# A two-layer decoder on one core: a broadcast product placed later in the list, one filling step kept back in the last attention group, and one weight conversion shared between two engines

## The chip, the cores and the metric

The kernel runs on one core of a Trainium2 chip. The core has a matrix engine (TensorE, PE in the views, with its weight loads as PEld), VectorE (DVE), ScalarE (ACT), GpSimd (POOL) and SyncE (SP), which only issues transfers here. Each engine runs its own list of instructions in order, and an instruction that waits for another engine holds up all that stands behind it in its list. The metric is the device time of one execution in microseconds (us), the median of several runs.

## The reference

The input is 256 tokens of 1024 features. Two layers follow each other, and each has an attention and a gated feed-forward part.

```python
for l in range(2):
    h = rmsnorm(x, attn_norm[l])              # x * rsqrt(mean(x*x) + eps) * gain
    # layer 0: q, k, v from w_qkv_a, 16 heads, causal attention over the block of 256
    # layer 1: 16 query heads, 4 shared key/value heads, window 128, a learned sink per head
    x = x + o @ w_o
    h = rmsnorm(x, ffn_norm[l])
    u = conv3(h @ w_up[l])                    # causal depthwise convolution of width 3
    gate, val = split(u)                      # 2816 columns each
    x = x + (silu(gate) * val) @ w_down[l]
out = rmsnorm(x, final_norm)
```

All arrays are float32, and so is the result.

## The kernel before

**Split products.** Every large product runs on parts: a value v becomes hi, its rounding to a shorter float32 form (fp32r), and lo = v - hi. Three matmuls (hi·hi, hi·lo, lo·hi) then stand for one. The small products of the attention, and the transposes, run on plain float32; each of those is shown as two matmuls in the trace (L486, L463 and L715 have twice as many there as the list has).

**Weights.** The weights are packed into units of 128 x 2048 values. Each is fetched by SP (`fetch`), ScalarE makes the high part (L157, `hi_part`) and VectorE the low part (L160, `lo_part`), in two or four pieces per unit. High and low parts have four buffers each, so unit i + 4 can only be converted when unit i has been used up: `used(i)` calls `prepare(i + 4)`, which puts the pieces into the planner. Units 55 to 58 are the output projection of layer 1; units 59 and up are the up-projection of its feed-forward part, of which 59 to 62 are converted while units 55 to 58 are being used up.

**The planner.** The list of instructions is written out in the order in which the code runs. A clock in nanoseconds counts matmul work: `tick(ns)` adds the cost of what was just written, and then runs all put-off steps that have come due. `chain(key, (delay, step), ...)` puts a step off until its delay has passed on that clock, counted from the step before it. `require(key)` runs the steps of a key at once, when something needs them.

**The order on the engines.** Up to L498 the list is taken as it stands for PE, ACT, DVE and SP. Behind that point (`manual.close()`), a scheduler walks over the list, and gives each engine the earliest instruction of the list whose operands and buffers are ready by its own reckoning. So an instruction whose operand is late slides behind a few of its successors, and one that is ready can be taken ahead of one that is not. The order that comes out is fixed; on the chip each engine goes through it and waits where it has to.

**The start.** `first_parts(c)` prepares chunk c (of eight) of the first product: one transfer brings 128 x 256 values of x and 128 x 512 of the weights. ScalarE makes x's high part (`hi`, L783), VectorE x's low part (`lo`, L786) and the weights' low part (`wl`, L787). The weights' high part (`wh`) is made by VectorE for chunk 0 (L782), and by ScalarE for the others (L785). `v_first(c)` then has six matmuls of 512 columns at L739: two with hi and wh, two with lo and wh, two with hi and wl. GpSimd works out the rotary angles at the same time (L764 and on).

**1 / rms for the feed-forward part.** Behind an attention, the sums of squares of the two halves b = 0, 1 of the tokens give r = 1 / rms per token (`rstd_of`, its power on GpSimd at L303). `row_bcast` has to turn this column into a row that is the same on all partitions: VectorE multiplies the unit matrix by r (L719), PE multiplies a matrix of ones with that (`spread`, L715), and ScalarE copies the result into `rb` (L717). Both layers do it, while PE is in the first two blocks of the up-projection (`ffn`, L627 to L629; three matmuls of 256 columns between two ticks of 320 ns). These first blocks use unscaled values; `rb` scales their results (L656) and the values that later blocks take (L640, then L642 and L643), from block 4 on.

**Attention.** `attention` handles four groups of four heads. Per group it writes the scores, the softmax, for each of two pairs the transposes of the probabilities (`probs_T`, L463, copied by VectorE at L471 and ScalarE at L469), and the product with the values (`values`, L486), whose result ScalarE splits at L492 and VectorE at L493. Between these it calls `fill(ns)`, which adds ns to a budget and takes steps from `filler` until the budget is used up. In layer 1 the filler is first the query projections of groups 1 to 3 (48 steps of 320 ns), then units 55 to 57 of the output projection (`Down.units`, 12 steps of 1280 ns, each of six matmuls of 512 columns: L533, L534, L538). `lead` and `rate(g)` are those budgets: 3500 ahead of the groups, then three numbers per group, ahead of the first transposes, ahead of the second, and behind them. What the filler still has behind the last group is written there. Then `finish` has unit 58, which needs the last group's L492 and L493, adds the result to x (L603), transposes it (L264), and scales and splits it (L276, L279, L280) for the feed-forward part.

Of the kernel before, what the change touches and what calls it, by code (L numbers as in the profile page):

```python
# [10 lines left out]
AF = mybir.ActivationFunctionType  # L11
# [5 lines left out]
S = 256  # L17
# [43 lines left out]
def trunk(ctx: ExitStack, tc, x, xw, pos, cpk, fin, sinks, w, out):  # L61
    nc = tc.nc
# [25 lines left out]
    def row3(n=3 * P):  # L88
        return wk.tile([P, 3 * P], F32, tag="m3", name=nm("m3"), bufs=8)[:, :n]

    def bank(tag):
        return ps.tile([P, 512], F32, tag=tag, name=nm(tag), bufs=4 if tag == "acc" else 2)

    def f(ap):
        return ap.bitcast(F32)

    def blk(b):
        return slice(b * P, (b + 1) * P)
# [17 lines left out]
    def tick(ns):  # L116
        clock[0] += ns
        while put_off and not busy[0]:
            item = min(put_off, key=lambda t: t[0])
            if item[0] > clock[0]:  # L120
                return
            run_item(item)

    def chain(key, *steps, urgent=0):

        def run(k):
            if urgent:
                with tc.high_priority(offset=urgent):
                    steps[k][1]()
            else:  # L130
                steps[k][1]()
            if k + 1 < len(steps):
                put_off.append((clock[0] + steps[k + 1][0], key, lambda: run(k + 1)))
        put_off.append((clock[0] + steps[0][0], key, lambda: run(0)))
# [67 lines left out]
    def chunk(c):  # L202

        t, at = (first[c // 2], KC * (c < 2) + c % 2 * CH) if c < 6 else (first[c - 3], 0)
        return t[:, at:at + S], t[:, at + S:at + CH]
# [90 lines left out]
    def rstd_of(b):  # L296

        require("sq", b)
        st = sums[b]
        r = wk.tile([P, 1], F32, tag="rstd", name=nm("rstd"), bufs=6)  # L300
        nc.vector.tensor_tensor(out=st[:, 2:3], in0=st[:, 0:1], in1=st[:, 1:2], op=ALU.add)
        nc.vector.tensor_scalar(out=st[:, 3:4], in0=st[:, 2:3], scalar1=1.0 / D, scalar2=EPS, op0=ALU.mult, op1=ALU.add)
        nc.gpsimd.tensor_tensor(out=r, in0=st[:, 3:4], in1=mhalf, op=ALU.pow)  # L303
        return r

    def hx(hT, c):
        hi, lo = hT[c // 4]
        return hi[:, c % 4], lo[:, c % 4]
# [399 lines left out]
    def row_bcast(rb, b):  # L708

        r = rstd_of(b)  # L710
        d = row3(P)

        def spread():
            t = bank("t")
            nc.tensor.matmul(t[:, :P], ones, d, start=True, stop=True)  # L715
            tick(450)
            chain(("rb", b), (200.0, lambda: nc.scalar.activation(rb[:, blk(b)], t[:, :P], AF.Copy)))  # L717

        chain(("rb", b), (2000.0, lambda: nc.vector.tensor_scalar(out=d, in0=ident, scalar1=r, scalar2=None, op0=ALU.mult)),  # L719
              (300.0, spread))  # L720

    manual = ExitStack()
    manual.enter_context(tc.manual_schedule(engines={mybir.EngineType.PE, mybir.EngineType.Activation,
# [53 lines left out]
    def first_parts(c):  # L777
        hi, lo = hx(hT, c)
        (src, raw), g = chunk(c), (g1 if c > 1 else g0)[:, c:c + 1]
        wh, wl = (t[:, (c % 4) * 512:(c % 4 + 1) * 512] for t in wq[c // 4])  # L780
        if c == 0:
            nc.vector.tensor_copy(wh, raw)  # L782
        nc.scalar.activation(hi, src, AF.Copy, scale=g)  # L783
        if c > 0:
            nc.scalar.activation(wh, raw, AF.Copy)  # L785
        nc.vector.scalar_tensor_tensor(out=lo, in0=src, scalar=g, in1=f(hi), op0=ALU.mult, op1=ALU.subtract)  # L786
        nc.vector.tensor_tensor(out=wl, in0=raw, in1=f(wh), op=ALU.subtract)  # L787

    warm_up(8)
    for c in range(4):  # L790
        first_parts(c)
        v_first(c)
        if c % 2:
            fetch(2 + c // 2)
    for b in range(NB):
        nc.sync.dma_start(xr[b], x[blk(b)])
    for c in range(4, KC):
        first_parts(c)
        if c < KC - 1:
            v_first(c)  # L800
# [51 lines left out]
    mask = one.tile([P, S], F32, name="mask")  # L852
# [12 lines left out]
    qk = {}  # L865
# [49 lines left out]
    def after_a(b, n):  # L915
        chain(("sq", b), (1500.0, lambda: square(b, n)))
        if n == 1:
            chain(("rb", b), (1500.0 + 700.0, lambda: row_bcast(rb, b)))
        feats(b, n, [(hT, G_FFN[0])], ("x", b, n), y)
# [27 lines left out]
    qk = {}  # L947
# [5 lines left out]
    def q_group(g):  # L953
        q = quad()
        for b in range(NB):
            o = bank("acc")[:, :256]
            yield from proj(o, qT_h, b, cols256(U_QB + g), (U_QB + g,) if b else ())
            rotate(o, 2, b, q[:, 0:2], q[:, 2:4], ("qk", g), lambda t, b=b, o=o: q_out(t, b, o))
        qk[g] = (q[:, 0:2], q[:, 2:4], kT[:, 0:2], kT[:, 2:4], lambda p: g // 2, lambda p: diagonal(0)(g // 2))
# [4 lines left out]
    def filler_b():  # L964
        for g in range(1, 4):
            yield from q_group(g)
        yield from o_down[0].units(0, 3)
# [1 line left out]
    def ready_b(oT):  # L969
        o_down.append(Down(U_OB, 4, oT, lambda i: require("o", i)))  # L970

    attention(qk, ready_b, filler_b(), 3500.0, lambda g: ((4200.0, 2200.0, 1400.0), (3200.0, 1800.0, 1200.0), (3200.0, 1800.0, 1200.0), (4000.0, 1800.0, 1500.0))[g], mask, lambda h: 2 * (h // 8) + h % 2, True)

    hT = new_hT()
    y = [quad(F32, "y") for _ in range(2)]
# [1 line left out]
    def after_b(b, n):  # L977
        chain(("sq", b), (1500.0, lambda: square(b, n)))
        if n == 1:
            chain(("rb", b), (1500.0 + 700.0, lambda: row_bcast(rb, b)))  # L980
        feats(b, n, [(hT, G_FFN[1])], ("x", b, n), y)
# [138 lines left out]
```

## Time and profile before

| what | us |
|---|---|
| runs before | 571.11, 571.14, 572.1 |
| median | 571.14 |
| the profiled execution, its own time | 570.39 |
| its span from the first to the last instruction | 568.3 |
| PE busy | 558.8 |
| DVE busy | 427.1 |
| ACT busy | 380.0 |
| POOL busy | 100.3 |

The span leaves out about 2 us around the instructions. The views of the trace count time from the span's start. PE is the engine that is busy nearly all the time; a stretch in which it waits is seen in the list of its instructions as a start that comes later than the pace of its neighbours.

### The profile page before, as it was taken

The numbers are of one execution on the slowest core, as the hardware profiler recorded it, in microseconds if no ns is written. First come the engines' busy times: TensorE is split into PE (matmuls) and PEld (weight loads), VectorE is DVE, ScalarE is ACT, GpSimd is POOL, SyncE is SP. The second block draws the span as 40 slices with busy tenths as digits, with TensorE's granted clock in tenths as the row PEclk, the third lists the DMA queues.
The fourth block names the chain that finished last, engine by engine and source line by source line (L and its number), as shares of the span: only waits on it lengthen the run. The fifth ranks groups of instructions, "written<-read, shape, count | busy, mean of one in ns | idle before, by whom it ended". The sixth has DMA issues, their size and how long they took to land.

```text
span 568.3 us, 10191 instructions
## 1 busy us (share of the span) xinstructions
PE 558.8 (98%) x3858; PEld 504.5 (89%) x3858; DVE 427.1 (75%) x927; ACT 380.0 (67%) x768; POOL 100.3 (18%) x124
## 2 busy tenths in 40 slices
PE   8999999999999999999999999999999999999995
PEld 7888888899999999988888988879999999988884
DVE  6798678599788888744469988788898888773414
ACT  6988777578577776743449798877667777663313
POOL 7321001011333321100002200001333332110003
PEclk9999999999999999999999999999999999999999
DMA  8974344442565565664542714242466655565201
GB/s 326 374 277 154 144 148 149 149 149 76 213 216 202 206 211 213 217 203 177 219 148 96 276 76 149 74 149 76 149 223 223 221 206 198 230 221 205 92 0 74
DMA packets 15311, 100.99 MB, mean 178 GB/s; under 512 B 1952, under 2 KB 2080, under 8 KB 3744
## 3 DMA queue, kind: packets, MB, share of 16 engines
q1 hardware_dynamic: 14976, 100.09, 48.4%
q8 instruction: 30, 0.49, 0.3%
q10 hardware_dynamic: 288, 0.26, 0.1%
q14 instruction: 17, 0.14, 0.1%
HBM read 99.30 MB, written 1.05 MB: 177 GB/s over the span
## 4 chain that ended last, share of the span: by engine, by line
PE 88%; DVE 5%; ACT 4%; issue 1%; POOL 1%; DMA 1%; DVEq 0%; POOLq 0%; ACTq 0%
PE acc L533 9%; PE acc L538 9%; PE acc L534 9%; PE u L628 6%; PE u L629 6%; PE u L627 6%; PE t L628 6%; PE t L629 6%; PE t L627 6%; PE acc L317 4%; PE acc L319 4%; PE acc L318 4%; PE acc L739 2%; PE acc L628 2%; PE acc L629 2%; PE acc L627 2%
## 5 line engine op out<-in xcount | busy, mean ns | idle before, releaser
L160 DVE TENSOR_TENSOR wl<-wr,wh 128x1024 fp32r<-128x1024 f32 (+1 forms) x208 | 221.0, 1080 | 68.1 <-ACT wh L157 67.7
L157 ACT ACTIVATE wh<-wr 128x1024 fp32r<-128x1024 f32 (+1 forms) x208 | 190.0, 946 | 75.0 <-PE acc L538 55.4
L533 PE MATMUL acc<-wh,q 128*128 128x512 f32 x238 | 94.5, 397 | 0.8 <-ACT q L492 0.7
L534 PE MATMUL acc<-wl,q 128*128 128x512 f32 x238 | 92.9, 390 | 0.0
L671 POOL TENSOR_TENSOR m<-m,m 128x256 f32<-128x256 f32 x44 | 60.2, 1367 | 182.2 <-DVE m L666 109.2
L628 PE MATMUL u<-q,wh 128*128 128x256 f32 x320 | 88.5, 277 | 0.0
L627 PE MATMUL u<-q,wh 128*128 128x256 f32 x320 | 88.2, 276 | 0.0
L629 PE MATMUL u<-q,wl 128*128 128x256 f32 x320 | 88.1, 275 | 0.0
L629 PE MATMUL t<-q,wl 128*128 128x256 f32 x288 | 79.2, 275 | 0.0
L627 PE MATMUL t<-q,wh 128*128 128x256 f32 x288 | 79.2, 275 | 0.0
L628 PE MATMUL t<-q,wh 128*128 128x256 f32 x288 | 79.2, 275 | 0.0
L538 PE MATMUL acc<-wh,q 128*128 128x512 f32 x238 | 76.9, 389 | 0.0
L628 PEld LDWEIGHTS u<-q,wh 128*128 128x128 f32 x320 | 60.1, 188 | 0.1
L627 PEld LDWEIGHTS u<-q,wh 128*128 128x128 f32 x320 | 60.0, 188 | 0.1
L629 PEld LDWEIGHTS u<-q,wl 128*128 128x128 f32 x320 | 60.1, 188 | 0.0
L317 PE MATMUL acc<-wh,q 128*128 128x512 f32 (+1 forms) x160 | 57.1, 357 | 0.0
L319 PE MATMUL acc<-wh,q 128*128 128x512 f32 (+1 forms) x160 | 55.4, 346 | 0.0
L318 PE MATMUL acc<-wl,q 128*128 128x512 f32 (+1 forms) x160 | 55.2, 345 | 0.0
L627 PEld LDWEIGHTS t<-q,wh 128*128 128x128 f32 x288 | 54.1, 188 | 0.0
L628 PEld LDWEIGHTS t<-q,wh 128*128 128x128 f32 x288 | 54.1, 188 | 0.0
L629 PEld LDWEIGHTS t<-q,wl 128*128 128x128 f32 x288 | 54.1, 188 | 0.0
L533 PEld LDWEIGHTS acc<-wh,q 128*128 128x128 f32 x238 | 44.7, 188 | 10.5 <-ACT q L492 1.6
(165 smaller groups left out, 995.1 us busy)
## 6 DMA issues: line engine op xcount, KB each, us to landing
wr<-in_w SPq DMA_DIRECT2D x90, 1024.0 KB, 4.8
first<-in_xw SPq DMA_DIRECT2D x5, 384.0 KB, 5.6
xr<-in_x SPq DMA_DIRECT2D x2, 512.0 KB, 8.3
first<-in_xw SPq DMA_DIRECT2D x1, 768.0 KB, 7.0
fin_t<-in_fin SPq DMA_DIRECT2D x1, 512.0 KB, 6.2
out<-ot SPq DMA_DIRECT2D x1, 512.0 KB, 2.6
first<-in_xw SPq DMA_DIRECT2D x1, 388.0 KB, 3.6
out<-m ACTq DMA_DIRECT2D x1, 256.0 KB, 2.1
```

What stands on the lines that cost most here:

```text
L157: nc.scalar.activation(wq[i][0][:, c], raws[i][:, c], AF.Copy)
L160: nc.vector.tensor_tensor(out=wq[i][1][:, c], in0=raws[i][:, c], in1=f(wq[i][0][:, c]), op=ALU.subtract)
L317: nc.tensor.matmul(o, xh[:, blk(b)], wh, start=(c == 0), stop=False)
L318: nc.tensor.matmul(o, xh[:, blk(b)], wl, start=False, stop=False)
L319: nc.tensor.matmul(o, xl[:, blk(b)], wh, start=False, stop=(c == KC - 1))
L533: nc.tensor.matmul(o, ph[:, blk(b)], hi[:, s_], start=first, stop=False)
L534: nc.tensor.matmul(o, ph[:, blk(b)], lo[:, s_], start=False, stop=False)
L538: nc.tensor.matmul(o, pl[:, blk(b)], hi[:, s_], start=False, stop=end)
L627: nc.tensor.matmul(o, hi[:, s_], xh, start=(c == 0), stop=False)
L628: nc.tensor.matmul(o, hi[:, s_], xl, start=False, stop=False)
L629: nc.tensor.matmul(o, lo[:, s_], xh, start=False, stop=(c == KC - 1))
L671: nc.gpsimd.tensor_tensor(out=h, in0=gs, in1=t[1], op=ALU.mult)
```

## The change

Three places change. In `row_bcast` the step that holds the product with the ones is put off by 1500 ns on the planner's clock behind the multiplication of the unit matrix, and not by 300 ns; this holds in both layers. In `first_parts` the high part of chunk 1's weights is made in two halves: columns 0 to 255 by ScalarE, columns 256 to 511 by VectorE, where the copy stands ahead of the two low parts of that chunk. In layer 1 the last group's three filling budgets become 3600, 1200 and 600 ns instead of 4000, 1800 and 1500 ns.

```diff
@@ row_bcast
         chain(("rb", b), (2000.0, lambda: nc.vector.tensor_scalar(out=d, in0=ident, scalar1=r, scalar2=None, op0=ALU.mult)),
-              (300.0, spread))
+              (1500.0, spread))
@@ first_parts
         if c == 0:
             nc.vector.tensor_copy(wh, raw)
         nc.scalar.activation(hi, src, AF.Copy, scale=g)
-        if c > 0:
+        if c == 1:
+            nc.scalar.activation(wh[:, :S], raw[:, :S], AF.Copy)
+            nc.vector.tensor_copy(wh[:, S:], raw[:, S:])
+        elif c > 1:
             nc.scalar.activation(wh, raw, AF.Copy)
         nc.vector.scalar_tensor_tensor(out=lo, in0=src, scalar=g, in1=f(hi), op0=ALU.mult, op1=ALU.subtract)
@@ attention of layer 1
-    attention(qk, ready_b, filler_b(), 3500.0, lambda g: ((4200.0, 2200.0, 1400.0), (3200.0, 1800.0, 1200.0), (3200.0, 1800.0, 1200.0), (4000.0, 1800.0, 1500.0))[g], mask, ...)
+    attention(qk, ready_b, filler_b(), 3500.0, lambda g: ((4200.0, 2200.0, 1400.0), (3200.0, 1800.0, 1200.0), (3200.0, 1800.0, 1200.0), (3600.0, 1200.0, 600.0))[g], mask, ...)
```

## Rows read from the trace of the kernel before

**Rows 1.** The page: the busy time of each engine in us, with its share of the span, and the chain of work that ended last by engine.

```profile
PE 558.8 (98%) x3858; PEld 504.5 (89%) x3858; DVE 427.1 (75%) x927; ACT 380.0 (67%) x768; POOL 100.3 (18%) x124
PE 88%; DVE 5%; ACT 4%; issue 1%; POOL 1%; DMA 1%; DVEq 0%; POOLq 0%; ACTq 0%
```

**Rows 2.** The chain of waits, over the whole span, the two longest of PE's behind the start: who waited for whom, us in total, how often, the longest.

```profile
PE acc L533 <- ACT q L492: 0.7, 1, 0.7
PE t L715 <- DVE m L719: 0.6, 2, 0.3
```

**Rows 3.** The timeline in layer 0 around the two products with the ones (L715): start us, duration us, engine, line, operation, tiles, shapes, count, and in brackets the idle time before it and what ended it.

```profile
122.14 1.12 POOL L303 TENSOR_TENSOR rstd<-st,mhalf 128x1 f32<-128x1 f32 x1 [0.38 <-DVE st L302]
122.32 0.28 PE L629 MATMUL acc<-q,wl 128*128 128x256 f32 x1
122.44 0.43 PE L715 MATMUL t<-m,ones 128*128 128x128 f32 x2
122.62 0.36 PE L627 MATMUL acc<-q,wh 128*128 128x256 f32 x1
...
123.18 0.28 PE L628 MATMUL u<-q,wh 128*128 128x256 f32 x1
123.30 0.29 DVE L719 TENSOR_SCALAR m<-ident,rstd 128x128 f32<-128x128 f32 x1 [0.45 <-POOL rstd L303]
123.74 0.46 PE L715 MATMUL t<-m,ones 128*128 128x128 f32 x2 [0.28 <-DVE m L719]
123.95 0.36 PE L629 MATMUL u<-q,wl 128*128 128x256 f32 x1
```

**Rows 4.** The timeline in layer 1 at the same place, columns as before.

```profile
386.02 0.28 PE L628 MATMUL acc<-q,wh 128*128 128x256 f32 x1
386.28 0.46 PE L715 MATMUL t<-m,ones 128*128 128x128 f32 x2
386.50 0.36 PE L629 MATMUL acc<-q,wl 128*128 128x256 f32 x1
...
387.06 0.28 PE L627 MATMUL u<-q,wh 128*128 128x256 f32 x1
387.18 0.29 DVE L719 TENSOR_SCALAR m<-ident,rstd 128x128 f32<-128x128 f32 x1 [0.44 <-POOL rstd L303]
387.61 0.46 PE L715 MATMUL t<-m,ones 128*128 128x128 f32 x2 [0.27 <-DVE m L719]
387.82 0.36 PE L628 MATMUL u<-q,wh 128*128 128x256 f32 x1
```

**Rows 5.** The timeline in layer 1's attention: the values of the last group but one (the first two rows), and the end of the last group, PE, ACT and DVE.

```profile
360.75 1.52 PE L486 MATMUL t<-m,v 128*64 128x256 f32 x16
362.20 0.49 PE L533 MATMUL acc<-wh,q 128*128 128x512 f32 x1
...
368.64 0.39 PE L533 MATMUL acc<-wh,q 128*128 128x512 f32 x1
370.00 0.81 PE L463 MATMUL u<-ident,m 128*128 128x128 f32 x6
370.20 1.15 ACT L157 ACTIVATE wh<-wr 128x512 fp32r<-128x512 f32 x2 [0.89 <-PE acc L538]
370.75 1.90 PE L486 MATMUL t<-m,v 128*64 128x256 f32 x16
371.00 2.57 DVE L160 TENSOR_TENSOR wl<-wr,wh 128x512 fp32r<-128x512 f32 x4
371.25 0.47 ACT L469 ACTIVATE m<-u 128x384 f32<-128x384 f32 x1
371.62 1.14 ACT L157 ACTIVATE wh<-wr 128x512 fp32r<-128x512 f32 x2
372.68 0.60 ACT L492 ACTIVATE q<-t 128x512 fp32r<-128x512 f32 x1
373.33 0.50 PE L533 MATMUL acc<-wh,q 128*128 128x512 f32 x1 [0.69 <-ACT q L492]
```

**Rows 6.** The timeline of the start, chunks 0 and 1: POOL, ACT, DVE and PE.

```profile
4.38 0.43 DVE L782 CAST wh<-first 128x512 fp32r<-128x512 f32 x1 [3.32 <-DMA first<-in_xw]
5.22 1.19 POOL L764 TENSOR_SCALAR rb<-rb 128x8 f32<-128x8 f32 x2
6.06 0.73 PE L739 MATMUL acc<-wl,q 128*128 128x512 f32 x2
6.10 0.62 ACT L785 ACTIVATE wh<-first 128x512 fp32r<-128x512 f32 x1
6.22 0.49 DVE L786 SCALAR_TENSOR_TENSOR q<-first,q 128x256 fp32r<-128x256 f32 x1 [0.22 <-ACT q L783]
6.75 0.69 DVE L787 TENSOR_TENSOR wl<-first,wh 128x512 fp32r<-128x512 f32 x1
6.77 1.18 PE L739 MATMUL acc<-wh,q 128*128 128x512 f32 x4
8.24 0.39 PE L739 MATMUL acc<-wh,q 128*128 128x512 f32 x1
```

**Rows 7.** Instructions by line: duration in ns as shortest, median and longest, and when the first and the last start.

```profile
L279 DVE CAST q<-y x16: 282/284/295, 114.2 to 384.2; 128x256 fp32r<-128x256 f32 x16
L717 ACT ACTIVATE rb<-t x4: 277/278/278, 122.9 to 388.1; 128x128 f32<-128x128 f32 x4
```

More of the change, by code (lines that the diff above doesn't have):

```diff
@@ L970, in ready_b @@
         o_down.append(Down(U_OB, 4, oT, lambda i: require("o", i)))
-    attention(qk, ready_b, filler_b(), 3500.0, lambda g: ((4200.0, 2200.0, 1400.0), (3200.0, 1800.0, 1200.0), (3200.0, 1800.0, 1200.0), (4000.0, 1800.0, 1500.0))[g], mask, lambda h: 2 * (h // 8) + h % 2, True)
+    attention(qk, ready_b, filler_b(), 3500.0, lambda g: ((4200.0, 2200.0, 1400.0), (3200.0, 1800.0, 1200.0), (3200.0, 1800.0, 1200.0), (3600.0, 1200.0, 600.0))[g], mask, lambda h: 2 * (h // 8) + h % 2, True)
     hT = new_hT()
```

## Prediction, made before the changed kernel ran

> **What bounds the kernel now.** I read the page first: PE is busy 98% of the span, and the chain that ended last runs through PE for 88% of its length [rows 1]. Time can then be won only where PE has nothing to do, or does something it needn't. So I read next the chain of waits for PE alone. Behind the start it names two places: L533, which waits 0.7 us once for the copy L492, and the product with the ones, L715, which waits 0.6 us in two instances for VectorE's L719 [rows 2]. These are small beside 571 us, and the list counts only what ends a wait, not what a late start costs the instructions behind it. So I read each place in the timeline and compare the distance between starts with the pace of an undisturbed neighbour: both layers around L715 [rows 3, 4], the end of layer 1's last attention group [rows 5], and the start, where PE is not yet fed [rows 6]. The three edits lie at exactly these places; whether each gives back its stall is the question.
>
> **Part 1: the product with the ones.** In layer 0 the starts in the undisturbed list are 0.12 us apart (122.32 to 122.44). The first product costs 122.62 - 122.32 - 0.12 = 0.18 us: the work itself and the change of type. The second costs 123.95 - 123.18 - 0.12 = 0.65 us, so 0.47 us of it is waiting. What it waits for is L719, which starts at 123.30, right behind GpSimd's power that took from 122.14 to 123.26 [rows 3]. In layer 1 the first costs 386.50 - 386.02 - 0.12 = 0.36 us and the second 387.82 - 387.06 - 0.12 = 0.64 us [rows 4], that is 0.18 and 0.46 us over an undisturbed one. Together 0.47 + 0.18 + 0.46 = 1.11 us of waiting.
>
> How much later does the product come? The up-projection ticks 320 ns for three matmuls. With 300 ns the step falls due one such triple behind L719's, with 1500 ns five triples behind it (1600 ns): four triples, 12 matmuls, later in the list. The second keeps its place one triple behind the first. In the compiled order of before the scheduler had already slid both back a little, for lack of their operand, by 3 and 5 matmuls in layer 0, so that on the engine the second moves by 12 - 5 = 7 matmuls at least, 7 x 0.12 = 0.84 us, and by 12 at most, 1.44 us. PE, which could have been at it at 123.30, is then there at 124.1; the operand, 0.15 us behind the end of L719 at 123.59, is there at 123.74. The margin is 0.3 to 0.4 us, in layer 1 the same or one matmul more. So all 1.11 us should go; bounded by 0 (the operand moves with PE) and 1.11 us.
>
> What is late next: the copies into `rb` (L717), by some 0.3 us for the second one, since the product itself starts at 124.1 and not at 123.74. Queued behind them on ScalarE and VectorE are L640, L642 and L656; their result is needed from block 4 of the up-projection, more than 10 us later (three blocks of 48 matmuls are between). No transfer and no queue of SP or POOL is passed. I cost it at nothing; the cover is those blocks, and it would have to shrink by 10 us.
>
> **Part 2: half of chunk 1's high weights on VectorE.** PE starts chunk 1 at 6.77, right behind ScalarE's `wh`, which runs from 6.10 to 6.72; PE's own work of chunk 0, two matmuls that started at 6.06, would let it go on at about 6.5 [rows 6]. ScalarE takes 0.62 us for 512 columns [rows 6] and 0.28 for 128 [rows 7]; on a line between them half the columns take 0.39 us. Then `wh` is whole at 6.5 instead of 6.72, if VectorE has its half by then. It stands idle for 0.22 us ahead of L786 [rows 6], and a conversion of 128 x 256 takes it 0.28 us [rows 7]: it delays L786 by under 0.1 us, and PE needs that only behind two matmuls. The low part (6.75 to 7.44) is needed behind four matmuls, 4 x 0.23 = 0.9 us after 6.55, at 7.45, so it costs at most 0.1 us. From 8.24 on PE is fed. Gain 0.2 us; bounds 0 and 6.77 - 6.51 = 0.26 us.
>
> GpSimd runs two instructions from 5.22 to 6.41, right where VectorE's new copy would start (about 6.0); the only such conversion that the start shows, at 4.38, took 0.43 us while GpSimd was between instructions [rows 6], so no row shows one that starts in the middle of GpSimd's work; what it costs if it has to wait is a rival below. The Trainium skill (SBUF — State Buffer, "SBUF: two separate sides") says that a one-source float32 copy of VectorE and any GpSimd instruction take a shared pair of ports for their whole length, and that whoever comes second is blocked until the first ends. By that rule the start would lose 0.15 us, where the rows let it win 0.2; by the length of L786 and L787 beside GpSimd the trace does not speak for it.
>
> **Part 3: a filling step behind the last values.** The budgets add up to 27700, 29500 and 31000 ns in the last group. 15360 go to the query projections; the rest, in steps of 1280, is 10, 12 and 12 steps (a step is taken while any budget is left). With the new numbers (27300, 28500, 29100) it is 10, 11 and 11. So ahead of the first transposes nothing changes, ahead of the second one step instead of two is written, and the twelfth step, six matmuls or 370.00 - 368.64 = 1.36 us, stands behind the values.
>
> Undisturbed, the values take 362.20 - 360.75 = 1.45 us up to the next matmul. At the end of the last group it is 373.33 - 370.75 = 2.58 us: 1.13 us of waiting, part of it inside the values for L469 and 0.69 us behind them for L492 [rows 5]. Both copies are late since ScalarE first converts four pieces of unit 61 (370.20 to 371.35, 371.62 to 372.76), which became possible when step 12 had used up unit 57 (the wait of 0.89 us for L538). With the step behind the values, the transposes come at 368.64 and end at 369.39; ScalarE is free, L469 is done by about 369.95, while the first half of the values runs until 370.1; the values end at 370.85, L492 at 371.5, L493 at 372.2, and step 12 covers 370.85 to 372.2. Then `finish` starts at 372.2 instead of 373.33, and unit 61 is converted behind that, while ScalarE would idle.
>
> That holds if the scheduler leaves the step where the list has it. It may put some of its matmuls between the halves of the values, where its reckoning sees a gap. If it puts all six there, the wait for L492 remains and only the 0.44 us inside the values, less 0.11 us for one more change of type (0.50 us for the L533 at 373.33, which follows plain float32, and 0.39 for the one at 368.64 [rows 5]), is won: 0.33 us. I take 0.9 us, near the upper end, since in the row of the group before the values ran without a gap; bounds are given by these and the last rival below.
>
> What is late next: the conversions of unit 61, four of 0.52 us on ScalarE and four of 0.6 us on VectorE, and its follow-up transfer, by 2 us. Unit 61 is used from block 2 of the up-projection, some 20 us later; VectorE's first add L603 could stand behind one low part, 0.6 us, which moves the transposes behind it by less than that. I cost it at nothing, with 0.6 us as the bound.
>
> **The sum**, against the profiled execution: 570.39 - 1.11 - 0.2 - 0.9 = 568.18 us. The median of the runs is 0.75 us above that execution, so 571.14 - 2.21 = 568.9 us.
>
> **Rivals.** A measurement of this kernel can tell about 0.2%, 1.14 us, from no change.
> - The step is put between the halves of the values. For it: the scheduler fills every gap it sees. Against: the copies take about as long as the first half of the values. 571.14 - 1.11 - 0.2 - 0.33 = 569.5 us.
> - VectorE's copy is held up by GpSimd until 5.22 + 1.19 = 6.41, 0.4 us. The low parts behind it are late by as much: the second comes at 7.85 for a PE that wants it at 7.65, and chunk 2 starts at 8.40 instead of 8.05. For it: the overlap at 6.0; against: L786 and L787 keep their length beside GpSimd [rows 6]. 568.9 + 0.35 = 569.3 us. This is the mechanism that the page named above describes.
> - The products gain nothing: if L719 comes later too, or the scheduler slides L715 by itself to where it was (it may give it the place in which its operand is ready, so the list's place decides only where it lies behind that). Then only parts 2 and 3 are left: 571.14 - 1.1 = 570.0 us; with part 3 at 0.33 us, 570.6 us.
> - Slower: ScalarE's list keeps unit 61's pieces ahead of L469 and L492, as it had them. Then step 12 must stand in front of the second half of the values, and ends at 369.39 + 0.72 + 1.36 = 371.5; two pieces end at 372.65, L469 at 373.05, the values' second half at 373.8, two more pieces end at 374.1, L492 at 374.65: 1.3 us later than before. With VectorE's low pieces ahead of L493 (0.2 us) and the change of type (0.1 us) it is 1.6 us: 571.14 - 1.31 + 1.6 = 571.4 us. It decides from 1.31 us on, which is what the other parts give. For it: this is the order in rows 5; against: L469 and L492 are earlier in the list, and unit 61's pieces no longer come free ahead of them.
>
> **How the numbers follow.** The forecast has a chance of 0.55, the step between the halves 0.15, the copy behind GpSimd 0.08, no gain from the products 0.12, the slower case 0.10. Predicted is 568.9 us. The range takes in the first four: from 571.14 - 1.11 - 0.26 - 1.13 = 568.6, and 0.4 us less for the spread of the runs, to 570.6: 568.2 to 570.6 us. Faster by over 0.2% (below 570.0) are the first three and a part of the fourth, 0.76; within 0.2% the rest of the fourth and most of the slower case, 0.19; slower by over 0.2% only if the slower case costs 2.45 us, 0.05.
>
> **What would show it.** In the profile after, PE's wait for L719 is gone, and the matmul behind each L715 starts 0.3 us behind the one ahead of it. L739's chunk 1 starts at 6.55, chunk 2 at 8.05. The matmuls of a filling step stand between the last L486 and `finish`, L492 starts within 0.2 us of the end of L486, and the conversions of unit 61 stand behind L492. It would be wrong if the waits only move: to L264 for late adds, to a block 2 that waits for unit 61, or to L715 again because GpSimd's power shifts with PE.

## The result: 568.15 us, faster by 0.56%

| | before | after |
|---|---|---|
| median of the runs on one chip | 571.12 us | 568.15 us |
| lowest and highest | 571.02, 572.1 | 567.93, 568.26 |
| the profiled execution, its own time | 570.39 us | 567.93 us |
| its span | 568.3 us | 565.9 us |

The ratio is 0.9944 with a 95% interval of 0.9926 to 0.9961: 2.97 us less. The forecast was 568.9 us with a range of 568.2 to 570.6, so the direction is right and the range was missed by 0.05 us at its lower end. In two later comparisons on other chips (e5, e9) the same kernel took 568.07 and 568.36 us, 2.78 and 2.30 us under the kernel before. So the same change measures 2.30 to 2.97 us, and the miss of 0.05 us is smaller than this scatter.

The page of after, the lines that answer to [rows 1]: busy time by engine, and the chain that ended last.

```profile
PE 558.0 (99%) x3858; PEld 504.4 (89%) x3858; DVE 427.7 (76%) x928; ACT 379.6 (67%) x768; POOL 101.6 (18%) x124
PE 93%; ACT 3%; DVE 3%; issue 1%; POOL 0%; DVEq 0%; POOLq 0%; ACTq 0%
```

PE has as much work as before (3858 matmuls); its share of the chain rose from 88% to 93%, because other engines hold it up less. The chain of waits of after, all of PE's behind the start:

```profile
PE t L358 <- DVE m L352: 0.4, 1, 0.4
PE acc L533 <- ACT q L492: 0.2, 1, 0.2
```

Of [rows 2] the wait for L719 is gone, and so is the 0.7 us for L492. The 0.2 us that the list names for L492 lie at another place, 353.38 us, where PE stands between the same two matmuls for as long as before (0.52 us from start to start, 0.51 before). The wait for L352 is in the list of before too, with the same 0.4 us. The timeline of after around L715 in layer 0 answers to [rows 3]:

```profile
123.23 0.29 DVE L719 TENSOR_SCALAR m<-ident,rstd 128x128 f32<-128x128 f32 x1 [0.44 <-POOL rstd L303]
...
123.83 0.28 PE L629 MATMUL u<-q,wl 128*128 128x256 f32 x1
123.95 0.38 PE L715 MATMUL t<-m,ones 128*128 128x128 f32 x2
124.09 0.36 PE L627 MATMUL u<-q,wh 128*128 128x256 f32 x1
```

L719 comes at the old time (123.23, before 123.30) and PE now reaches the second product at 123.95, 0.43 us behind the end of L719 at 123.52. This product costs 124.09 - 123.83 - 0.12 = 0.14 us over its neighbours' pace. The first one of layer 0 costs 0.13 us, and the two of layer 1, where [rows 4] show the stall before, 0.13 and 0.14.

The timeline of after at the end of layer 1's last group, PE and ACT, answers to [rows 5]:

```profile
368.21 0.81 PE L463 MATMUL u<-ident,m 128*128 128x128 f32 x6
368.95 1.52 PE L486 MATMUL t<-m,v 128*64 128x256 f32 x16
369.06 0.49 ACT L469 ACTIVATE m<-u 128x384 f32<-128x384 f32 x1 [0.19 <-PE u L463]
370.40 0.50 PE L533 MATMUL acc<-wh,q 128*128 128x512 f32 x1
370.52 0.60 ACT L492 ACTIVATE q<-t 128x512 fp32r<-128x512 f32 x1 [0.97 <-PE t L486]
...
371.89 0.39 PE L533 MATMUL acc<-wh,q 128*128 128x512 f32 x1
372.09 1.68 ACT L157 ACTIVATE wh<-wr 128x512 fp32r<-128x512 f32 x3 [0.97 <-PE acc L538]
```

The values take 370.40 - 368.95 = 1.45 us, the undisturbed length, where they took 2.58. The kept step runs from 370.40, `finish` from 371.89, and ScalarE does L469, L492 and only then unit 61 (L157 at 372.09).

The start of after, answering to [rows 6]: PE at chunks 0, 1, 2, 4 and 5, ScalarE's first work on chunk 4, and VectorE's new copy (the CAST at L786) beside GpSimd.

```profile
4.92 1.46 PE L739 MATMUL acc<-wh,q 128*128 128x512 f32 x4
5.19 1.20 POOL L764 TENSOR_SCALAR rb<-rb 128x8 f32<-128x8 f32 x2
5.89 0.29 DVE L786 CAST wh<-first 128x256 fp32r<-128x256 f32 x1
6.22 0.63 PE L739 MATMUL acc<-wl,q 128*128 128x512 f32 x2
6.68 1.07 PE L739 MATMUL acc<-wh,q 128*128 128x512 f32 x4
8.05 1.08 PE L739 MATMUL acc<-wh,q 128*128 128x512 f32 x4
9.67 0.51 ACT L783 ACTIVATE q<-first,g 128x256 fp32r<-128x256 f32 x1 [0.85 <-DMA first<-in_xw]
10.78 1.16 PE L739 MATMUL acc<-wh,q 128*128 128x512 f32 x4
12.24 1.07 PE L739 MATMUL acc<-wh,q 128*128 128x512 f32 x4
```

Chunk 4 in the timeline of before, ScalarE and PE:

```profile
9.69 0.51 ACT L783 ACTIVATE q<-first,g 128x256 fp32r<-128x256 f32 x1 [0.86 <-DMA first<-in_xw]
10.96 1.08 PE L739 MATMUL acc<-wh,q 128*128 128x512 f32 x4
```

Chunk 2 starts at 8.05 (before 8.24), as forecast. But ScalarE's first work on chunk 4 still begins at 9.67 (before 9.69), behind a transfer, and PE loses 0.1 us again between chunks 4 and 5 (1.46 us apart instead of 1.36).

### The profile page after: what moved, and what is told of

Its sections match the earlier page's. It is cut to its first block, busy times and chain, and to the rows that moved or that the text cites. A ratio compares the mean times of both kernels' runs of the same rounds, so it can differ in the third digit from the quotient of the medians.

```text
span 565.9 us, 10192 instructions
## 1 busy us (share of the span) xinstructions
PE 558.0 (99%) x3858; PEld 504.4 (89%) x3858; DVE 427.7 (76%) x928; ACT 379.6 (67%) x768; POOL 101.6 (18%) x124
## 4 chain that ended last, share of the span: by engine, by line
PE 93%; ACT 3%; DVE 3%; issue 1%; POOL 0%; DVEq 0%; POOLq 0%; ACTq 0%
PE acc L533 9%; PE acc L534 9%; PE acc L538 9%; PE u L628 6%; PE u L627 6%; PE u L629 6%; PE t L628 6%; PE t L629 6%; PE t L627 6%; PE acc L317 4%; PE acc L319 4%; PE acc L318 4%; PE acc L739 2%; PE acc L627 2%; PE acc L628 2%; PE acc L629 2%
## 5 line engine op out<-in xcount | busy, mean ns | idle before, releaser
L157 ACT ACTIVATE wh<-wr 128x1024 fp32r<-128x1024 f32 (+1 forms) x208 | 189.8, 946 | 69.7 <-PE acc L538 55.5
L671 POOL TENSOR_TENSOR m<-m,m 128x256 f32<-128x256 f32 x44 | 64.7, 1470 | 176.3 <-DVE m L666 129.0
```

What stands on the lines that cost most here:

```text
L157: nc.scalar.activation(wq[i][0][:, c], raws[i][:, c], AF.Copy)
L671: nc.gpsimd.tensor_tensor(out=h, in0=gs, in1=t[1], op=ALU.mult)
```

## Experiments

The theory: the three stalls are where the gain is, and the terms of the sum hold. The rival for the first four runs: the usual execution waits longer at these places than the one that was profiled, by the 0.75 us between that execution and the median.

**e1_products, e2_start, e3_fill, e4_plain**: one part of the change each, put alone into the kernel before, and the kernel before itself.

```diff
e1_products
-              (300.0, spread))
+              (1500.0, spread))
e2_start
-        if c > 0:
+        if c == 1:
+            nc.scalar.activation(wh[:, :S], raw[:, :S], AF.Copy)
+            nc.vector.tensor_copy(wh[:, S:], raw[:, S:])
+        elif c > 1:
e3_fill
-    attention(... (4000.0, 1800.0, 1500.0) ...)     # the last group's budgets
+    attention(... (3600.0, 1200.0, 600.0) ...)
```

> Only the two products with the ones are put off (1500 instead of 300 ns), in both layers. Theory A, the terms of the sum are right and only the 0.75 us between the profiled execution of before and its median was no property of the kernel: 1.1 to 1.2 us faster than before, L715 has no wait left, and the profile's span shortens by about as much. Theory B, a usual execution of before waits longer at these products than the profiled one did, since the power on GpSimd takes longer there: 1.7 to 1.9 us faster.

> Only half of chunk 1's high weights is made by VectorE. Theory A: 0.2 us faster, chunk 2's first matmul at about 8.05 instead of 8.24 us. Theory B, the transfers of the start land later in a usual execution, and the shared conversion hides that: 0.5 us or more. If VectorE's copy had to wait for GpSimd: 0.1 to 0.2 us slower.

> Only the last filling step stands behind the last values. Theory A: 1.0 to 1.3 us faster; the values take 1.45 us up to the next matmul. Theory B, a usual execution of before waits longer in front of the last unit than the profiled one: 1.7 us or more.

> The kernel before, unchanged, once more. Theory A: same as before within 0.1%; its profiled execution lies within 0.8 us of its median on either side, so the distance between one profiled execution and the median is scatter, and the starts at L715 and L533 repeat within 0.2 us of those of the first profile. Theory B: the profiled execution shows more waiting at one of the three places than the first profile did, about 0.6 us in all.

Measured on one chip, where the kernel before took 570.87 us:

| run | median us | ratio, 95% | less than before |
|---|---|---|---|
| e1_products | 569.55 | 0.9977 [0.9968, 0.9986] | 1.32 |
| e2_start | 570.83 | 0.9998 [0.9989, 1.0007] | 0.04 |
| e3_fill | 569.44 | 0.9976 [0.9967, 0.9985] | 1.43 |
| e4_plain | 570.69 | 0.9999 [0.9990, 1.0008] | 0.18 (the same kernel) |

The products and the filling step measure a little over the 1.1 to 1.2 and 1.0 to 1.3 us that were expected. The times alone do not exclude the rival: their intervals reach from 0.80 to 1.83 us for e1 and from 0.86 to 1.88 for e3, and the rival's 1.7 us lies in both. What speaks against it is that the stalls repeat. In e4, the kernel before, the four products cost 0.18, 0.65, 0.34 and 0.65 us over the pace (the first profile: 0.18, 0.65, 0.36 and 0.64), and the last values take 373.49 - 370.90 = 2.59 us up to the next matmul (2.58):

```profile
373.49 0.50 PE L533 MATMUL acc<-wh,q 128*128 128x512 f32 x1 [0.69 <-ACT q L492]
```

The 0.18 us of the unchanged kernel is a difference between equal kernels, and the intervals are about 0.5 us on either side. The parts add up to 1.32 + 0.04 + 1.43 = 2.79 us.

For the start 0.2 us was forecast, and nothing can be seen. In e2's profiled execution chunk 2 came at 8.83 us, not at 8.05 as expected. There TensorE's clock rose late (at 6.91 us, where it rose at 4.14 in the first profile), and the first four matmuls of chunk 0 took 6.99 - 5.20 = 1.79 us instead of 1.11. The lines around chunk 1 in e2_start:

```profile
6.27 0.40 ACT L785 ACTIVATE wh<-first 128x256 fp32r<-128x256 f32 x1
7.46 1.07 PE L739 MATMUL acc<-wh,q 128*128 128x512 f32 x4
```

ScalarE is done at 6.67. Had it made all the columns, in 0.62 us, it would have been done at 6.89, still ahead of PE at 7.46. In such an execution the shared conversion has nothing to give.

**e5_all, e6_nostart**: the whole change, and the whole change with chunk 1's high weights on ScalarE again (the edit of e2 undone), together with e7 and e8 on one chip, where the kernel before took 570.85 us.

> The changed kernel as it is, on the chip of the runs beside it. If the three parts simply add, it stands 1.32 + 0.04 + 1.43 = 2.8 us below the kernel before (the sum of the three taken alone). If the shared conversion is worth its 0.2 us only when PE is not held up elsewhere, it is 3.0 us or more.

> The changed kernel without the shared conversion: ScalarE makes all of chunk 1's high weights again. If the shared conversion is worth the 0.2 us that was forecast, this is 0.2 us slower than the whole change; if its gain is lost in what the start does anyway (how early PE's clock rises, when the first transfers land), the two are within 0.1 us.

e5 took 568.07 us (567.93 to 569.97), e6 568.11 (567.99 to 568.16): the same, as the second theory of e6 has it. The profiles show two places at which the start's gain can go. PE and ScalarE at chunks 2 to 5 in e5_all:

```profile
7.89 1.07 PE L739 MATMUL acc<-wh,q 128*128 128x512 f32 x4
9.25 1.07 PE L739 MATMUL acc<-wh,q 128*128 128x512 f32 x4
9.78 0.51 ACT L783 ACTIVATE q<-first,g 128x256 fp32r<-128x256 f32 x1 [0.82 <-DMA first<-in_xw]
10.20 0.61 ACT L788 ACTIVATE wh<-first 128x512 fp32r<-128x512 f32 x1
10.86 1.19 PE L739 MATMUL acc<-wh,q 128*128 128x512 f32 x4
12.34 1.07 PE L739 MATMUL acc<-wh,q 128*128 128x512 f32 x4
```

and in e6_nostart, without the shared conversion, from chunk 1's weights on:

```profile
6.03 0.62 ACT L785 ACTIVATE wh<-first 128x512 fp32r<-128x512 f32 x1
6.44 0.62 PE L739 MATMUL acc<-wl,q 128*128 128x512 f32 x2
6.90 1.08 PE L739 MATMUL acc<-wh,q 128*128 128x512 f32 x4
...
8.27 1.07 PE L739 MATMUL acc<-wh,q 128*128 128x512 f32 x4
9.76 0.51 ACT L783 ACTIVATE q<-first,g 128x256 fp32r<-128x256 f32 x1 [0.84 <-DMA first<-in_xw]
10.98 1.07 PE L739 MATMUL acc<-wh,q 128*128 128x512 f32 x4
12.35 1.07 PE L739 MATMUL acc<-wh,q 128*128 128x512 f32 x4
```

At chunk 2 e5 is 0.38 us ahead, at chunk 5 0.01. The first place is chunk 4. In both kernels its data is there at about 9.77; PE can begin it 1.08 us later, when ScalarE's two conversions are done. In e6 PE arrives at 10.98 by its own pace. In e5 it would be there at 9.25 + 1.36 = 10.61 and stands until 10.86. The DMA issues of the profile show why the data is late: chunks 4 and 5 come in one transfer of 768 KB, the others in transfers of about 384 KB.

The second place is the clock. It rose at 4.25 us in e5 and at 6.08 in e6, so the first four matmuls of chunk 0 took 1.11 us in e5 and 1.57 in e6, and the lead of 0.38 us is not the shared conversion's alone. In e6 ScalarE's conversion for chunk 1 was done at 6.03 + 0.62 = 6.65, and PE came to it at 6.90, by its own work: here, as in e2, the conversion was not what PE waited for. The clock rose before 4.4 us in 6 of the 14 traces and at 5.54 us or later in 8. How much of the missing 0.2 us goes at which place in a usual run is not shown.

**e7_two_steps**: two steps kept for behind the values.

```diff
-    attention(... (3600.0, 1200.0, 600.0) ...)
+    attention(... (3600.0, 0.0, 0.0) ...)
```

> The whole change with last budgets of 3600, 0 and 0: two filling steps are kept for behind the values instead of one. If one step of 1.36 us covers the copies, as the 0.2 us that PE still waits for L492 says, a second can win 0.2 us at most. If the additional gain of part 3 (1.4 us measured, 0.9 forecast) comes from how much work stands behind the values, it wins another 0.3 us or more. If the steps ahead of the transposes had a cover to give, it loses.

568.73 us (568.52 to 568.77), 0.66 us slower than e5. The third case of the expectation came. (The 0.2 us of L492 that it counts on lie at another place, 353 us, see e12.) The timeline of PE:

```profile
367.27 1.11 PE L463 MATMUL u<-ident,m 128*128 128x128 f32 x6
368.31 1.80 PE L486 MATMUL t<-m,v 128*64 128x256 f32 x16
370.05 0.49 PE L533 MATMUL acc<-wh,q 128*128 128x512 f32 x1
```

The last transposes and the values take 370.05 - 367.27 = 2.78 us against 2.19 in after (368.21 to 370.40). The step ahead of the transposes had a cover to give: with two matmuls ahead of them instead of six, the transposes take 0.30 us longer (1.04 instead of 0.74) and the values 0.29 (1.74 instead of 1.45), together 0.59 of the 0.66 us. Of the splits that were run, one step on each side is the best.

**e8_p900**: the whole change, with the product put off by 900 ns.

```diff
-              (1500.0, spread))
+              (900.0, spread))
```

> The whole change with the product put off by 900 ns instead of 1500: on PE it stands 6 matmuls (0.72 us) earlier. If the operand's time is fixed by GpSimd and VectorE, PE comes to the second product about 0.4 us before it: 0.4 us of waiting in each layer come back, and the kernel is 0.8 us slower than the whole change. If any place behind the old one is as good, it is the same.

569.17 us (568.96 to 569.41), 1.10 us slower than e5. VectorE and PE around the second product of layer 0:

```profile
123.34 0.28 PE L629 MATMUL u<-q,wl 128*128 128x256 f32 x1
123.41 0.29 DVE L719 TENSOR_SCALAR m<-ident,rstd 128x128 f32<-128x128 f32 x1 [0.44 <-POOL rstd L303]
123.84 0.46 PE L715 MATMUL t<-m,ones 128*128 128x128 f32 x2 [0.23 <-DVE m L719]
124.06 0.36 PE L627 MATMUL u<-q,wh 128*128 128x256 f32 x1
```

It costs 124.06 - 123.34 - 0.12 = 0.60 us instead of 0.14; 0.44 us more in layer 1 too. That makes 0.90 of the 1.10 us, where 0.8 was expected. The first theory of the expectation holds: the operand's time is fixed (L719 starts at 123.41 here, 123.23 in after, 123.30 before), the place on PE decides, and 6 matmuls are all the difference. The scheduler does not slide the product to where its operand is ready.

**e9_all_again, e10_split, e11_split_nostart, e12_g2**, on a third chip, where the kernel before took 570.66 us. e10 fetches chunks 4 and 5 in two transfers, e11 does that without the shared conversion.

```diff
e10_split, e11_split_nostart
-    get_chunks(4, 2)
+    get_chunks(4)
+    get_chunks(5)
e12_g2
-    attention(... (3200.0, 1800.0, 1200.0), (3600.0, 1200.0, 600.0) ...)     # the last two groups' budgets
+    attention(... (2500.0, 2500.0, 1200.0), (3600.0, 1200.0, 600.0) ...)
```

> The changed kernel once more, to stand beside the next three on their chip: 2.7 to 2.9 us below the kernel before.

> The whole change, and chunks 4 and 5 of the first product are fetched in two transfers instead of one. Theory: the shared conversion does make PE early (up to 0.4 us at chunk 2), but chunk 4 cannot be converted before 9.75 us, when the transfer that holds chunks 4 and 5 has landed whole; PE waits there until 10.8, with or without the shared conversion. Then chunk 4 alone lands about 0.5 us earlier or more, PE goes from chunk 3 to chunk 4 without a wait, and the whole change gains 0.2 to 0.4 us. Rival: the wait only moves to a later chunk, since the transfers as a whole are the limit of the start: the same time as e9 within 0.1 us.

> The same split transfer without the shared conversion. Theory of the landing: PE comes to chunk 4 no earlier than 10.9 us by its own pace, so the split gives nothing here (within 0.1 us of the whole change), and the difference to the run before it, 0.2 to 0.4 us, is what the shared conversion is worth once the landing does not cap it. Rival: both split kernels take the same time.

> The whole change, with the budgets of layer 1's third group 2500, 2500 and 1200 instead of 3200, 1800 and 1200: its first filling step, which needs a copy of the group before, comes a step later in the list. In the whole change PE stands for 0.4 us at 352.9 us, where that first step's product follows a matmul of the scores by plain order. If that stand is for the copy, the kernel wins 0.3 to 0.4 us; if it is only a change of type or a weight load, it is the same.

| run | median us | lowest, highest |
|---|---|---|
| e9_all_again | 568.36 | 567.95, 568.46 |
| e10_split | 568.68 | 568.51, 568.71 |
| e11_split_nostart | 568.87 | 568.63, 569.44 |
| e12_g2 | 568.11 | 567.83, 568.35 |

e9 is 2.30 us below the kernel before, where 2.7 to 2.9 was expected: a miss, though the interval of this comparison reaches from 1.83 to 3.25 us.

The timeline of e10_split, PE at chunks 2, 4 and 5, ScalarE at chunk 4, and the last transfer (its lines are numbered one higher than those of after):

```profile
8.12 1.07 PE L740 MATMUL acc<-wh,q 128*128 128x512 f32 x4
8.66 0.51 ACT L784 ACTIVATE q<-first,g 128x256 fp32r<-128x256 f32 x1
10.84 1.07 PE L740 MATMUL acc<-wh,q 128*128 128x512 f32 x4
12.20 1.07 PE L740 MATMUL acc<-wh,q 128*128 128x512 f32 x4
562.76 0.34 SPq L1032 DMA_DIRECT2D out<-m  x1
```

The theory of the landing holds: with a transfer of its own chunk 4 is converted from 8.66, 1.1 us earlier, and PE keeps its pace of 1.36 us through chunks 2 to 5. The Trainium skill (DMA: Bandwidth & Descriptors, "Why a DMA increments its semaphore by 16 and not by 1") says that only a transfer's full count means that all its data landed. e5 and e10 agree: chunk 4 is converted from 9.78 us where it shares a transfer of 768 KB with chunk 5, and from 8.66 with a transfer of its own.

But the times are misses. e10 is 0.32 us slower than e9, where 0.2 to 0.4 us faster was expected, and e11 is 0.51 us slower, where the same time within 0.1 us was expected. In e10 the last matmul does start 0.29 us earlier than in e9 (559.58 against 559.87; 0.12 us of it at chunk 5 already, 12.20 against 12.32), and the execution ends 0.2 us later. From the issue of the last output transfer (562.76, in e9 563.05) to the end of the span it is 3.75 us in e10 and 3.78 in e11, and 3.25 to 3.27 in the twelve traces without the added transfer. So the kernels with the added transfer end 0.5 us later behind their last output transfer; why stays open.

What the shared conversion is worth once the landing does not cap it is not settled either. The medians of e10 and e11 differ by 0.19 us, about the 0.2 to 0.4 expected, but their ranges overlap, and the two profiles differ in the clock: TensorE goes from the lower of its two levels (1.2 GHz) to the upper (2.4 GHz) at 4.37 us in e10 and at 6.65 us in e11, and the four first matmuls of chunk 0 took 6.15 - 5.05 = 1.10 us in e10 and 6.74 - 4.95 = 1.79 us in e11. In both PE had run the same warm-up matmuls from 1.11 us on.

e12 is a miss. Its 0.25 us lie within the spread. PE waits at the same place for the same copy, in e12_g2 as here and in e9_all_again at 353.78 for 0.15 us:

```profile
353.75 0.50 PE L533 MATMUL acc<-wh,q 128*128 128x512 f32 x1 [0.16 <-ACT q L492]
```

The step was written later in the list, but the scheduler took its matmul from there to the same slot on PE: the matmuls from 350 us up to this one have the same order in both.

## Why the prediction was right, and where it failed

**What bounds the kernel** was right: all that was won is PE's standing time, with the same work. The mechanism of parts 1 and 3 was right too; what failed are the sizes of their terms, and in part 2 the claim that PE is fed behind chunk 2.

**Part 1** was right in mechanism and nearly in margin (forecast: PE 0.3 to 0.4 us behind the operand; PE is there at 123.95, the operand at 123.52 + 0.15 = 123.67). Its 1.11 us were too small. The four products cost 0.18, 0.65, 0.36 and 0.64 us over the pace before, and 0.13, 0.14, 0.13 and 0.14 after, which is 1.29 us; e1 measured 1.32. The step that failed is the one that takes layer 0's first product, at 0.18 us, as undisturbed. A product that waits for nothing costs 0.13 to 0.14 us, so each of the four gave 0.04 to 0.05 us more, and the 1.11 us were no upper bound.

**Part 2** failed at the sentence "From 8.24 on PE is fed". Half the columns took ScalarE 0.40 us (estimated 0.39), the copy took VectorE 0.29, and chunk 2 came at 8.05. That this is the forecast number to the digit is luck: chunk 1 came at 6.68 and not at 6.55, since the first four matmuls took 1.30 us instead of 1.11, and then took 1.37 us instead of 1.50. Chunk 4's landing at 9.7 left PE no more than 0.2 us before (it came at 10.96 and could have come at 9.69 + 1.08 = 10.77), and the rows of the start that were read [rows 6] stop ahead of it. The working also takes for granted that ScalarE's conversion is what PE waits for at chunk 1, which was not so in the profiled executions of e2 and e6, where TensorE's clock rose late. Worth: 0.2 forecast, 0.04 measured alone (e2) and 0.04 on top of the other two (e6).

**Part 3**: the order is the forecast one. The 0.9 us were taken as a discount on 1.13 us, for a step that might be put between the halves of the values; none was, and all 1.13 us came (2.58 to 1.45). The discount is the step that failed here. e3 measured 1.43, and its trace shows where some of the rest comes from. Over the same number of matmuls (111), from the one at 368.64 to the one at 386.02 [rows 4, 5], the kernel before takes 17.38 us, e3 16.23 (369.54 to 385.77) and after 16.21 (368.21 to 384.42): about 1.16 us less, 0.03 more than the stall. In e3 PE then comes to layer 1's first product when its operand is already there:

```profile
385.99 0.28 PE L629 MATMUL acc<-q,wl 128*128 128x256 f32 x1
386.11 0.41 PE L715 MATMUL t<-m,ones 128*128 128x128 f32 x2
386.27 0.36 PE L627 MATMUL acc<-q,wh 128*128 128x256 f32 x1
```

It costs 386.27 - 385.99 - 0.12 = 0.16 us, where it cost 0.36. These 0.20 us are won by part 1 as well, so parts 1 and 3 overlap by them, and the sum of the parts counts them twice.

**The sum.** From the trace of before to that of after, the start of the last matmul moves from 561.83 to 559.48 us, by 2.35 us: 0.09 at the start, 1.29 for the products and 1.16 for the step, which is 2.54 us, less 0.2 us that are lost in layer 1's attention between 314 and 368 us. That stretch is 0.3 us longer in e2 too, whose code there is that of before; what makes it vary is open. So the terms of the forecast, 2.21 us, were about 0.3 us short (0.18 in part 1 and 0.26 in part 3, less 0.1 in part 2). The rest of the 2.97 us is not accounted for by any row; the two later comparisons have 2.78 and 2.30. Taking the gain off the median of the runs was no mistake, but the 0.75 us between the profiled execution and the median are no property of the kernel: the distance is 0.22 us for after, 0.14 for e4_plain and -0.47 for e3_fill. The lower end of the range was built from bounds that were not bounds (1.11 for the products, 1.13 for the step); with 1.29 and 1.16 it would have been 0.2 us lower and held the time.

**The rivals.** The step between the halves, and unit 61 ahead of L469 and L492, did not come. Nor did the copy held up by GpSimd: it runs from 5.89 to 6.18 in the middle of L764 (5.19 to 6.39) and in its usual length, so the rule of the Trainium skill's page SBUF — State Buffer ("SBUF: two separate sides") that the prediction weighed did not show here. "The products gain nothing" fell with e1 and e8. Two figures of the working do not follow: the chances of the first three cases add up to 0.78, so "faster by over 0.2%" should have had at least that and not 0.76; and in the rival of the copy, a low part at 7.85 and two matmuls of 0.23 us give chunk 2 at 8.3, not 8.40.

## What to carry to other kernels

A gain at one chunk of a pipeline is kept only up to the next point that is set from outside: look in the timeline for the next wait on a transfer, and see how much earlier the engine that bounds the kernel may arrive there. Work put behind a late copy pays until the place that it was taken from becomes uncovered; count both sides. And a bound made from "undisturbed" rows is one only if nothing waits in those rows. Two parts that were measured alone can share a gain: see in the traces whether the same wait goes away in both.

## What the hardware showed that was not expected

The moment at which TensorE's clock rises is not repeatable. With the same warm-up matmuls from 1.11 us on, the records of the granted clock reach the upper level (2.4 GHz) at 4.00 us in e4_plain, 4.25 in e5_all, 5.54 in after, 6.08 in e6_nostart and 6.91 in e2_start. The four first matmuls of chunk 0 take 1.1 us in the six executions in which it rises before 4.4 us, and 1.3 to 1.9 us in the eight in which it rises at 5.5 to 6.9. That is up to 0.7 us at the start, more than the edit there was to bring, though the wait for chunk 4 swallows part of it.
